# Two-step batches of VectorE's small work in a kernel's expert-row stage, with GpSimd's product ordered behind each batch

## The chip, the cores and the metric

The kernel runs on one core of one Trainium2 chip. The metric is the device time of one execution in microseconds (us); lower is better. The profile is one execution of its own, and its stretches are counted from the start of its span.

## The reference

The program is two transformer blocks, one after the other, on 256 tokens of width 2048, in 32-bit floats. The change lies in the feed-forward part of the first block, a mixture of 16,384 very small experts (`peer`). Each token has eight heads. A head has 128 scores for each of two key halves; it keeps the 16 best of each half, forms the 256 sums, and keeps the 16 best pairs. That gives 16 expert numbers and 16 gates (a softmax) for each of 256 tokens and eight heads. An expert is one row of 2048 numbers in `expert_down` and one in `expert_up`:

```python
expert_idx = jnp.take_along_axis(cand_i.reshape(T, H, K * K), best_pos, axis=-1)
gates = jax.nn.softmax(best_s, axis=-1).astype(x.dtype)
u = expert_down[ib]
act = jax.nn.gelu(jnp.einsum('td,thkd->thk', xb, u), approximate=False)
vv = expert_up[ib]
return jnp.einsum('thk,thkd->td', gb * act, vv)
```

So every token needs 128 rows of `expert_down`, a dot product of each with the token's own vector, a gelu, a multiplication by the gate (the result is called the coefficient here), and then a weighted sum of 128 rows of `expert_up`. The rest of the program (attention, retention, a second block with a grouped mixture of experts) is not touched.

## The kernel before, in words

128 tokens lie on the 128 partitions, so there are two token tiles (t = 0 and 1). The **down stage** is one Python loop of 128 steps `s`; a step is two of the sixteen experts of one head of one token tile, that is two down rows per token. The first 64 steps belong to tile 0, the other 64 to tile 1, eight steps to a head. Four streams of work meet in the loop.

- **Gathers** (`down_gather`, L628, on GpSimd's queue, POOL in the profile): two indirect DMAs per step, each bringing one row of 8 KB per token, 1 MB in all, into half of a buffer of the pool `big`. Step s issues the rows for three steps ahead (two after step 58). A gather waits until its buffer's last user is done.
- **Dot products** (`down_dots`): most rows go to VectorE (DVE), which multiplies a row by the token vector `hnp`, kept in PSUM, and sums it in one custom instruction (L669). In every second step (s even) the second row (numbers 1, 5, 9 and 13 of a head, `POOL_ROWS`) goes to GpSimd instead: it multiplies the row by the vector's copy `hn` in SBUF (L666), and ScalarE (ACT) sums the product later (`row_sum`, L642). Two steps, four rows, thus have one GpSimd product and three VectorE dots. Steps 0 to 7 and step 64 have no GpSimd product.
- **Routing** (`route`, L579 to L621): for each tile and head about 25 small VectorE instructions and one ScalarE exponential find the 16 experts. They are cut into eight pieces, 128 pieces for the 16 heads. `route_to(17 + int(ROUTE * s))` issues 1.41 pieces per step, so the last is issued near step 78.
- **Coefficient chunks** (`store_coefs`, 32 pieces from step 65 on): the coefficients of tile 0 are spread out to a table over experts. A piece takes four tokens: ScalarE builds one-hot rows (L694, L695), VectorE builds the coefficient side (`ab`, four instructions, L713), TensorE multiplies the two (L715), ScalarE copies the result (L716). Every eighth piece fills a chunk; three of the four are stored by a DMA that ScalarE issues (L767), and the chunk's buffer is one of those that rows use. `onehots_ahead` builds 28 more groups of one-hot rows on ScalarE from step 85 on. Per head ScalarE also takes the gelu (L646), and VectorE multiplies by the gates (L647).

In the program, step s calls gather, dots, then `settle` (work put off from the step before: the row sum, a head's coefficients), then its routing pieces and its piece of the tables. The text order is not the order on an engine: a scheduler fills each engine's queue by its own estimate of when an instruction can run. `tc.issue_after(x)` holds what follows back until instruction x has been issued in that order; it is no wait on the chip. Each engine then runs its own queue strictly in order, so an instruction that waits holds up all behind it. After the loop come the tables of tile 1 and the **up stage**, bound by TensorE.

Of the kernel before, what the change touches and what calls it, by code (L numbers as in the profile page):

```python
# [15 lines left out]
ALU = mybir.AluOpType  # L16
# [50 lines left out]
UA = 3  # L67
NC0 = 1
POOL_ROWS = (1, 5, 9, 13)
ROUTE = 1.41  # L70


def bc_rows(ap, n):
# [4 lines left out]
def build(ctx: ExitStack, tc: tile.TileContext, A, out, taps=None, stop=None):  # L78
    nc = tc.nc
    V, S, G, TE = nc.vector, nc.scalar, nc.gpsimd, nc.tensor  # L80
# [9 lines left out]
    env = {}  # L90
# [14 lines left out]
    def raw_tile(shape, name):  # L105
        p_ = env["raw"][env["ri"] % len(env["raw"])]
        env["ri"] += 1
        return p_.tile(shape, F32, tag="raw", name=name)
# [19 lines left out]
    def e8(shape, dt=F32, name="e8"):  # L128
        return env["wk"].tile(shape, dt, tag="e8", name=name, bufs=env["e8"])

    def bigt(shape, dt=F32, name="b"):
        return big.tile(shape, dt, tag="big", name=name)
# [175 lines left out]
    def pst(name="pst"):  # L308
        return pt.tile([P, 512], F32, tag="t", name=name)
# [171 lines left out]
    for b in range(4):  # L481
        ps = proj(5632 + b * 512)
        sg = w4([P, 2, 512], name="sg")
        for t in range(2):
            S.activation(sg[:, t, :], ps[:, t, :], AF.Silu, scale=r1[:, t:t + 1])
            V.tensor_tensor(out=ret[:, t, b * 512:(b + 1) * 512], in0=ret[:, t, b * 512:(b + 1) * 512],
                            in1=sg[:, t, :], op=ALU.mult)
# [62 lines left out]
    hn = bigt([P, 2, D], name="hn")  # L550
# [76 lines left out]
    def gather(dst, src, idx):  # L627
        G.indirect_dma_start(out=dst, out_offset=None, in_=src, in_offset=bass.IndirectOffsetOnAxis(ap=idx, axis=0))  # L628

    late = []  # L630

    def settle(n):

        while late and late[0][0] <= n:
            late.pop(0)[1]()

    def put_off(n, fn):
        late.append((n, fn))
        late.sort(key=lambda e: e[0])

    def row_sum(prod, dst):
        S.activation(prod, prod, AF.Copy, accum_out=dst)  # L642

    def peer_coefs(t, hd, dots):
        c_ = coef[:, t, hd * 16:(hd + 1) * 16]
        S.activation(c_, dots, AF.Gelu)  # L646
        V.tensor_tensor(out=c_, in0=c_, in1=gates[:, t, hd, :], op=ALU.mult)  # L647

    def down_gather(s):

        t, hd, k = s // 64, s // 8 % 8, s % 8 * 2
        row = bigt([P, 2, D], name="row")
        for i in range(2):
            gather(row[:, i, :], dn_d, eidx[:, t, hd, k + i:k + i + 1])
        rows[s] = row

    def down_dots(s, hnp):

        t, hd, k = s // 64, s // 8 % 8, s % 8 * 2
        if k == 0:  # L660
            rows["dots"] = sm.tile([P, 16], F32, tag="dots", name="dots")
        row, dots = rows.pop(s), rows["dots"]
        for i in range(2):
            r_, d_ = row[:, i, :], dots[:, k + i:k + i + 1]
            if hnp is not None and k + i in POOL_ROWS:
                G.tensor_tensor(out=r_, in0=r_, in1=hn[:, t, :], op=ALU.mult)  # L666
                put_off(s + 1, lambda r_=r_, d_=d_: row_sum(r_, d_))
            else:
                env["dot"] = V.tensor_tensor_reduce(out=r_, in0=r_, in1=hn[:, t, :] if hnp is None else hnp, scale=1.0,  # L669
                                                    scalar=0.0, op0=ALU.mult, op1=ALU.add, accum_out=d_)  # L670
        if k == 14:
            put_off(s + 1, lambda: peer_coefs(t, hd, dots))

    def key_rows(t):

        ps = pst("pky")
        for i in range(2):
            TE.transpose(ps[:, i * P:(i + 1) * P], ijf[:, t, i, :], ident)
        kT = env["wk"].tile([P, 2, P], F32, tag="brow", name="kT")
        V.tensor_copy(kT, ps[:, 0:2 * P].rearrange("p (a t) -> p a t", a=2))  # L680
        return kT
# [8 lines left out]
    def onehots(dst, kT, tk, n):  # L690


        for i in range(n):
            S.activation(dst[:, i, :], iota, AF.Square, scale=-1.0, bias=kT[:, 1, tk + i:tk + i + 1])  # L694
        S.activation(dst, dst, AF.Relu, scale=-1.0, bias=1.0)  # L695
# [46 lines left out]
    hnp = psum.enter_context(tc.tile_pool(name="hp", bufs=1, space=PSUM, reuse_waits="tile")).tile([P, D], F32, name="hnp")  # L742
    routed = [0]
# [9 lines left out]
    def route_to(n):  # L753

        while routed[0] < min(n, 128):
            next(route_pieces)
# [4 lines left out]
    def store_coefs():  # L761
        kT, cT = key_rows(0), coef_rows(0)
        for c in range(4):
            for cc_ in coef_chunk(kT, cT, c):
                yield
            if c < 4 - NC0:
                nc.scalar.dma_start(ct_d[c], cc_.rearrange("p i t -> p (i t)"))  # L767
            else:
                c0.append(cc_)

    def onehots_ahead(kT, oh1):

        for n, mk in ((16, lambda: raw_tile([P, 16, P], "oh1")), (16, lambda: raw_tile([P, 16, P], "oh1")),
                      (16, lambda: raw_tile([P, 16, P], "oh1")), (8, lambda: ws0.tile([P, 8, P], F32, tag="hi", name="oh1")),
                      (8, lambda: ws0.tile([P, 8, P], F32, tag="lo", name="oh1")),
                      (8, lambda: ws0.tile([P, 8, P], F32, tag="hi", name="oh1")),
                      (8, lambda: ws0.tile([P, 8, P], F32, tag="lo", name="oh1")),
                      (16, lambda: e8([P, 16, P], name="oh1")), (16, lambda: e8([P, 16, P], name="oh1"))):
            tk = 4 * len(oh1)
            o_ = mk()  # L780
            for q in range(0, n, 4):
                onehots(o_[:, q:q + 4], kT, tk + q, 4)
                oh1.append(o_[:, q:q + 4])
                yield

    kT1, oh1 = None, []
    stored = ahead = iter(())
    issued = 0
    route_to(16)
    for s in range(128):  # L790
        while issued < min(128, s + (4 if s < 58 else 3)):
            down_gather(issued)
            issued += 1
        if s in (6, 64):
            S.copy(hnp, hn[:, s // 64, :])
        down_dots(s, None if s < 8 or s == 64 else hnp)
        if s == 64:
            stored = store_coefs()
        settle(s)
        with tc.issue_after(env["dot"].ins):  # L800
            route_to(17 + int(ROUTE * s))
            if s > 64 and s % 3:
                next(stored, 1)
            if kT1 is None and routed[0] == 128:
                kT1 = key_rows(1)
                ahead = onehots_ahead(kT1, oh1)
            if s > 84 and s % 4:
                next(ahead, 1)
    settle(1000)
    for bg in (stored, ahead):  # L810
        for _ in bg:
# [454 lines left out]
    for pr in range(2):  # L1266
# [3 lines left out]
        for t in range(2):  # L1270
            for g in range(2 * pr, 2 * pr + 2):
# [5 lines left out]
                    in1=oh[:, :, :, None].to_broadcast([P, 2, 4, 8]), op=ALU.mult)  # L1277
# [261 lines left out]
```

## Time and profile before

| | us |
|---|---|
| median of 3 runs | 3273.74 |
| lowest and highest of them | 3271.95, 3275.97 |
| the profiled execution's own time | 3273.31 |
| its span | 3271.5 |
| VectorE busy | 2539.7 (78%) |
| GpSimd busy | 901.2 (28%) |
| ScalarE busy | 1659.8 (51%) |
| TensorE busy | 2553.7 (78%) |

The span in 40 slices of 82 us shows the down stage as the gap in TensorE's row: from about 900 to 1640 us TensorE is nearly idle, and GpSimd is busy nowhere else. Each digit is the busy share of a slice in tenths.

```
PE   9999999999800002222099999999999999999999
DVE  6665555455999999979788888888566699999984
ACT  5534444444422224673254444458444677777773
POOL 0000000000476775566776666640000000000000
DMA  7455555565898998899879999984654499999964
```

In such rows PE is TensorE, DVE VectorE, ACT ScalarE, POOL GpSimd; a row of the timeline gives start, duration, engine, line, operation and, in brackets, the engine's idle time just before and what ended it.

### The profile page before, as it was taken

To read this page: it belongs to the slowest core of one execution; us is meant where nothing else is said; L and a number is where in the kernel's file an instruction comes from. 1 tells how busy PE (TensorE), PEld (TensorE's weight loads), DVE (VectorE), ACT (ScalarE), POOL (GpSimd) and SP (SyncE) were. 2 spreads that over 40 slices of the span, in tenths; PEclk is the share of its full clock that TensorE was granted. 3 is DMA by queue.
4 is the path that set the end of the run, shared out by engine and by line. 5 is a ranking of instruction groups with operands and counts; after the bars stand their busy time and mean duration, and the time that the engine had idled before them with its cause. 6 is when DMAs were issued, how large, how long until landed. Compare 5 with 4: busy or idle time off the path is not lost. (4 is left out here: it accounts for less than half of the span.)

```text
span 3271.5 us, 35254 instructions
## 1 busy us (share of the span) xinstructions
PE 2553.7 (78%) x12368; PEld 2142.2 (65%) x12368; DVE 2539.7 (78%) x3564; ACT 1659.8 (51%) x2334; POOL 901.2 (28%) x634
## 2 busy tenths in 40 slices
PE   9999999999800002222099999999999999999999
PEld 7788888888800001111088888889987787878777
DVE  6665555455999999979788888888566699999984
ACT  5534444444422224673254444458444677777773
POOL 0000000000476775566776666640000000000000
PEclk9999999999955555555599999999999999999999
DMA  7455555565898998899879999984654499999964
GB/s 241 154 168 169 191 189 189 203 204 193 333 388 345 366 352 315 313 360 343 353 250 335 335 333 333 335 289 164 198 168 161 173 335 350 374 350 381 348 235 167
DMA packets 302521, 898.20 MB, mean 275 GB/s; under 512 B 20736, under 2 KB 42240, under 8 KB 268288
## 3 DMA queue, kind: packets, MB, share of 16 engines
q1 hardware_dynamic: 226560, 542.88, 47.2%
q0 software_dynamic: 57760, 335.65, 27.1%
q10 hardware_dynamic: 18016, 17.35, 1.6%
q8 instruction: 98, 1.61, 0.2%
q14 instruction: 87, 0.71, 0.1%
HBM read 887.42 MB, written 8.39 MB: 274 GB/s over the span
## 5 line engine op out<-in xcount | busy, mean ns | idle before, releaser
L262 DVE TENSOR_TENSOR wlo<-raw,whi 128x1024 fp32r<-128x1024 f32 (+1 forms) x538 | 647.9, 1207 | 448.3 <-ACT whi L261 441.7
L261 ACT CAST whi<-raw 128x1024 fp32r<-128x1024 f32 (+1 forms) x538 | 558.6, 1040 | 680.8 <-PE pj L292 255.9
L669 DVE CUSTOM_DVE_ANT_0 row<-row,hnp 128x2048 f32<-128x2048 f32 x179 | 403.8, 2278 | 38.2 <-DMA row<-in_peer_expert_down_dram,eidx 37.9
L207 POOL TENSOR_TENSOR r<-rstdv,mhalf 128x2 f32<-128x2 f32 x5 | 4.4, 889 | 1509.5 <-DVE rstdv L233 1509.5
L628 POOL DMA_INDIRECT urow<-in_peer_expert_up_dram,eidx x256 | 322.0, 1258 | 196.1 <-DVE h L838 139.7
L628 POOL DMA_INDIRECT row<-in_peer_expert_down_dram,eidx x256 | 264.2, 1032 | 307.0 <-DVE dots L669 85.0
L262 DVE TENSOR_TENSOR wlo<-rawg,whi 128x1024 fp32r<-128x1024 f32 x256 | 313.0, 1224 | 37.2 <-ACT whi L261 12.7
L261 ACT CAST whi<-rawg 128x1024 fp32r<-128x1024 f32 x256 | 269.8, 1055 | 99.1 <-PE pgu L1351 69.5
L290 PE MATMUL pj<-whi,xhi 128*128 128x512 f32 x736 | 289.4, 393 | 1.3 <-ACT whi L261 1.3
L291 PE MATMUL pj<-wlo,xhi 128*128 128x512 f32 x736 | 288.9, 393 | 0.0
L292 PE MATMUL pj<-whi,xlo 128*128 128x512 f32 x736 | 288.2, 392 | 0.0
L715 PE MATMUL pcc<-ab 128*128 128x128 f32 x288 | 76.0, 434 | 253.7 <-DVE ab L713 226.7
L666 POOL TENSOR_TENSOR row<-row,hn 128x2048 f32<-128x2048 f32 x59 | 266.6, 4519 | 4.6 <-DMA row<-in_peer_expert_down_dram,eidx 3.5
L715 PEld LDWEIGHTS pcc<-ab 128*128 128x128 f32 x288 | 63.2, 314 | 266.5 <-issue 166.6
L1350 PE MATMUL pgu<-wlo,xs 128*128 128x512 f32 x512 | 200.1, 391 | 3.1 <-DVE wlo L262 3.1
L1349 PE MATMUL pgu<-whi,xs 128*128 128x512 f32 x512 | 200.3, 391 | 0.0
L1351 PE MATMUL pgu<-whi,xs 128*128 128x512 f32 x512 | 199.4, 390 | 0.0
L838 DVE SCALAR_TENSOR_TENSOR h<-urow,pk,h 128x512 f32<-128x512 f32 x256 | 191.6, 748 | 4.4
L685 PE MATMUL pcf<-cc,pk 128*128 128x128 f32 x2 | 0.9, 474 | 248.0 <-DVE pk L647 248.0
L642 ACT ACTIVATE row<-row 128x2048 f32<-128x2048 f32 x59 | 112.2, 1903 | 143.4 <-POOL row L666 143.4
L262 DVE TENSOR_TENSOR wlo<-rawd,whi 128x1024 fp32r<-128x1024 f32 x128 | 154.0, 1223 | 12.2 <-ACT whi L261 1.1
L685 PEld LDWEIGHTS pcf<-cc,pk 128*128 128x128 f32 x2 | 0.4, 180 | 248.7 <-DVE pk L647 248.7
(552 smaller groups left out, 6842.4 us busy)
## 6 DMA issues: line engine op xcount, KB each, us to landing
raw<-in_w_in_dram SPq DMA_DIRECT2D x124, 1024.0 KB
raw<-in_peer_expert_up_dram SPq DMA_DIRECT2D x96, 1024.0 KB
rawg<-in_w_expert_gate_dram SPq DMA_DIRECT2D x128, 512.0 KB
rawg<-in_w_expert_up_dram SPq DMA_DIRECT2D x128, 512.0 KB
rawd<-in_w_expert_down_dram SPq DMA_DIRECT2D x64, 1024.0 KB
raw<-in_w_out_dram SPq DMA_DIRECT2D x32, 1024.0 KB
raw<-in_w_ret_branch_dram SPq DMA_DIRECT2D x16, 1024.0 KB
raw<-in_w_peer_query_dram SPq DMA_DIRECT2D x16, 1024.0 KB
```

What stands on the lines that cost most here:

```text
L261: S.copy(hi, raw)
L262: env["last"] = V.tensor_tensor(out=lo, in0=raw, in1=hi.bitcast(F32), op=ALU.subtract)
L290: TE.matmul(ps[:, t, :], h_, hi, start=st, stop=False)
L291: TE.matmul(ps[:, t, :], h_, lo, start=False, stop=False)
L292: env["mm"] = TE.matmul(ps[:, t, :], l_, hi, start=False, stop=en)
L628: G.indirect_dma_start(out=dst, out_offset=None, in_=src, in_offset=bass.IndirectOffsetOnAxis(ap=idx, axis=0))
L666: G.tensor_tensor(out=r_, in0=r_, in1=hn[:, t, :], op=ALU.mult)
L669: env["dot"] = V.tensor_tensor_reduce(out=r_, in0=r_, in1=hn[:, t, :] if hnp is None else hnp, scale=1.0, scalar=0.0, op0=ALU.mult, op1=AL ...
L838: V.scalar_tensor_tensor(out=h[:, t, 1536:2048], in0=row[:, k, :], scalar=coef[:, t, c0 + k:c0 + k + 1], in1=h[:, t, 1536:2048], op0=ALU.m ...
L1349: TE.matmul(o_, xh, hi[:, :, i, :], start=k == 0, stop=False)
L1350: TE.matmul(o_, xh, lo[:, :, i, :], start=False, stop=False)
L1351: TE.matmul(o_, xl, hi[:, :, i, :], start=False, stop=k == NK - 1)
```

## The change

Five things. In every even step but the first, the routing pieces of two steps are issued together (`ROUTE` is doubled and taken at s/2), with the table pieces of two steps behind them, and none in odd steps. This batch is held back until the last dot and the newest ScalarE instruction have been issued. The dots of a step are moved to the end of the step, behind the batch, and held back until the newest VectorE instruction has been issued. The second row of a step comes ahead of the first. And GpSimd's product gets a wait, on the chip, for the VectorE instruction that is newest where it is written.

```diff
-ROUTE = 1.41
+ROUTE = 2.82
...
-        for i in range(2):
+        for i in (1, 0):
             r_, d_ = row[:, i, :], dots[:, k + i:k + i + 1]
             if hnp is not None and k + i in POOL_ROWS:
-                G.tensor_tensor(out=r_, in0=r_, in1=hn[:, t, :], op=ALU.mult)
+                g_ = G.tensor_tensor(out=r_, in0=r_, in1=hn[:, t, :], op=ALU.mult)
+
+                tc.add_manual_dep(g_.ins, newest(V).name, mybir.DependencyInfo(
+                    mybir.DependencyClass.Sync, mybir.DependencyReason.DATA), reason="shared port")
                 put_off(s + 1, lambda r_=r_, d_=d_: row_sum(r_, d_))
...
-        down_dots(s, None if s < 8 or s == 64 else hnp)
         if s == 64:
             stored = store_coefs()
         settle(s)
-        with tc.issue_after(env["dot"].ins):
-            route_to(17 + int(ROUTE * s))
-            if s > 64 and s % 3:
-                next(stored, 1)
-            if kT1 is None and routed[0] == 128:
-                kT1 = key_rows(1)
-                ahead = onehots_ahead(kT1, oh1)
-            if s > 84 and s % 4:
-                next(ahead, 1)
+        if s and s % 2 == 0:
+            with tc.issue_after(env["dot"].ins), tc.issue_after(newest(S)):
+                route_to(18 + int(ROUTE * s / 2))
+                if kT1 is None and routed[0] == 128:
+                    kT1 = key_rows(1)
+                    ahead = onehots_ahead(kT1, oh1)
+                if s > 64:
+                    next(stored, 1)
+                    if s % 3 == 0:
+                        next(stored, 1)
+                if s > 84:
+                    next(ahead, 1)
+                    if s % 4 == 0:
+                        next(ahead, 1)
+        with tc.issue_after(newest(V)):
+            down_dots(s, None if s < 8 or s == 64 else hnp)
```

`newest(eng)` returns the last instruction written so far for that engine. By the new line numbers the VectorE dot is L676, GpSimd's product L670, the row sum L646, the gate product L651, `ab` L720.

On VectorE, in the first half of the loop (an `ISA` row with `row,dots` is a dot of 2048 elements, the `dots` row behind it reads its sum). Before, the small work of a head stands in every gap but the one inside a step of two VectorE dots:

```order
L587 CAST if_7131<-i_7108 128x32
L595 MAX bv<-rtmp 128x8
L596 MAX_INDEX bp<-bv,rtmp 128x8
L597 MATCH_REPLACE rtmp<-bv,rtmp 128x256
L669 ISA row,dots<-row,hnp 128x2048
L669 ISA dots 128x1
L599 MAX bv<-rtmp 128x8
L600 MAX_INDEX bp<-bv,rtmp 128x8
L602 TENSOR_SCALAR ab<-bp 128x16
L603 TENSOR_SCALAR ab<-bp 128x16
L605 CAST abf<-ab 128x32
L669 ISA row,dots<-row,hnp 128x2048
```

Now three dots stand in a row between two batches:

```order
L603 TENSOR_SCALAR ab<-bp 128x16
L605 CAST abf<-ab 128x32
L608 TENSOR_TENSOR rtmp<-abf,cc 128x512
L610 TENSOR_TENSOR rtmp<-rtmp,if_7134 128x512
L676 ISA row,dots<-row,hnp 128x2048
L676 ISA dots 128x1
L676 ISA row,dots<-row,hnp 128x2048
L676 ISA dots 128x1
L676 ISA row,dots<-row,hnp 128x2048
L676 ISA dots 128x1
L613 TENSOR_REDUCE pk<-rtmp 128x2x16
L617 TENSOR_SCALAR nm<-bv 128x1
```

The small instructions that stood between the first and the second dot have moved out; the same count of them now runs in one stretch ahead of the three dots.

On GpSimd, in the same part, with the waits (DMASW is a gather's landing). Before, the product waits for its row alone:

```order
L628 DMA row<-in_peer_expert_down_dram,eidx 128x2048 [waits DMASW3_49,DVE_49]
L628 DMA row<-in_peer_expert_down_dram,eidx 128x2048 [waits DMASW4_49]
L666 TENSOR_TENSOR row<-row,hn 128x2048 [waits DMASW6_49]
L628 DMA row<-in_peer_expert_down_dram,eidx 128x2048 [waits DMASW5_49,Activation_49]
L628 DMA row<-in_peer_expert_down_dram,eidx 128x2048
```

Now:

```order
L628 DMA row<-in_peer_expert_down_dram,eidx 128x2048 [waits DMASW3_49,DVE_49]
L628 DMA row<-in_peer_expert_down_dram,eidx 128x2048 [waits DMASW4_49]
L670 TENSOR_TENSOR row<-row,hn 128x2048 [waits DMASW6_49,DVE_49]
L628 DMA row<-in_peer_expert_down_dram,eidx 128x2048 [waits DMASW5_49,Activation_49]
L628 DMA row<-in_peer_expert_down_dram,eidx 128x2048
```

The places of product and gathers are the same; the product has one more wait, for VectorE, and the four gathers behind it stand behind that wait too.

## Rows read from the trace of the kernel before

**Rows 1.** Busy time by stretch: start:end, length, each engine's busy us, TensorE's clock, DMA share, GB/s.

```profile
904.00:1197.00 293.00, 0.66 (x2) 0.29 (x2) 289.02 (x453) 68.03 (x83) 209.74 (x124) 0.50 0.93 360
1197.00:1333.00 136.00, 21.70 (x73) 16.97 (x73) 133.75 (x258) 54.12 (x104) 80.44 (x50) 0.50 0.84 324
1333.00:1565.00 232.00, 49.24 (x186) 41.64 (x186) 192.26 (x209) 131.75 (x307) 151.57 (x91) 0.50 0.89 344
1585.00:1610.00 25.00, 0.00 (x0) 0.00 (x0) 17.05 (x16) 5.44 (x6) 21.34 (x12) 0.50 1.01 424
```

**Rows 2.** Timeline of GpSimd: the products of steps 8, 58, 78, 114 and 126.

```profile
904.06 4.53 POOL L666 TENSOR_TENSOR row<-row,hn 128x2048 f32<-128x2048 f32 x1
...
1197.04 4.53 POOL L666 TENSOR_TENSOR row<-row,hn 128x2048 f32<-128x2048 f32 x1
...
1333.79 4.50 POOL L666 TENSOR_TENSOR row<-row,hn 128x2048 f32<-128x2048 f32 x1
...
1565.22 4.53 POOL L666 TENSOR_TENSOR row<-row,hn 128x2048 f32<-128x2048 f32 x1
...
1623.86 4.51 POOL L666 TENSOR_TENSOR row<-row,hn 128x2048 f32<-128x2048 f32 x1 [2.92 <-DMA row<-in_peer_expert_down_dram,eidx]
```

**Rows 3.** Timeline of VectorE and GpSimd: a product beside small work, and a gather.

```profile
1010.40 4.64 DVE L587 CAST if<-i 128x32 f32<-128x32 uint32 x1
1010.48 4.51 POOL L666 TENSOR_TENSOR row<-row,hn 128x2048 f32<-128x2048 f32 x1
...
1022.67 1.46 POOL L628 DMA_INDIRECT row<-in_peer_expert_down_dram,eidx  x1 [0.30 <-issue]
```

**Rows 4.** Groups of VectorE, 904 to 1197 us: count | busy us, mean ns | idle before.

```profile
L621 DVE TENSOR_SCALAR pk<-pk,nm 128x16 f32<-128x16 f32 x8 | 15.8, 1972 | 0.1
L602 DVE TENSOR_SCALAR ab<-bp 128x16 uint32<-128x16 uint32 x9 | 14.1, 1570 | 0.3
L608 DVE TENSOR_TENSOR rtmp<-abf,cc 128x512 f32<-128x512 f32 x9 | 12.8, 1417 | 0.2
L587 DVE CAST if<-i 128x32 f32<-128x32 uint32 x9 | 11.2, 1245 | 0.0
L590 DVE TENSOR_TENSOR rtmp<-v 128x256 f32<-128x256 f32 x9 | 10.3, 1145 | 0.0
L614 DVE SCALAR_TENSOR_TENSOR eidx<-pk 128x16 int32<-128x16 f32 x8 | 8.7, 1082 | 0.0
L610 DVE TENSOR_TENSOR rtmp<-rtmp,if 128x512 f32<-128x512 f32 x9 | 6.2, 692 | 0.3
...
L597 DVE MATCH_REPLACE8 rtmp<-bv,rtmp 128x256 f32<-128x256 f32 x9 | 3.7, 409 | 0.0
L603 DVE TENSOR_SCALAR ab<-bp 128x16 uint32<-128x16 uint32 x9 | 1.7, 185 | 0.0
```

**Rows 5.** One line each, the dot and `ab`: ns min/median/max, first and last start.

```profile
L669 DVE CUSTOM_DVE_ANT_0 row<-row,hnp x179: 2262/2278/2289, 899.6 to 1628.7; 128x2048 f32<-128x2048 f32 x179
...
L713 DVE TENSOR_SCALAR ab<-cc,kT,cT x224: 322/340/5298, 1243.8 to 1664.5; 128x128 f32<-128x128 f32 x112
```

**Rows 6.** Groups of VectorE, 1197 to 1333 us.

```profile
L713 DVE TENSOR_SCALAR ab<-cc,kT,cT 128x128 f32<-128x128 f32 x37 | 24.0, 686 | 0.0
```

**Rows 7.** Groups of VectorE, 1333 to 1565 us.

```profile
L669 DVE CUSTOM_DVE_ANT_0 row<-row,hnp 128x2048 f32<-128x2048 f32 x53 | 119.3, 2278 | 18.0 <-DMA row<-in_peer_expert_down_dram,eidx 17.9
L713 DVE TENSOR_SCALAR ab<-cc,kT,cT 128x128 f32<-128x128 f32 x92 | 67.9, 800 | 0.0
...
L647 DVE TENSOR_TENSOR pk<-pk 128x16 f32<-128x16 f32 x5 | 4.7, 942 | 21.7 <-ACT pk L646 19.5 <-ACT row L642 2.2
```

**Rows 8.** Timeline of GpSimd: a gather behind a chunk's store, and the second gather of step 126.

```profile
1493.88 0.95 POOL L628 DMA_INDIRECT row<-in_peer_expert_down_dram,eidx  x1 [14.75 <-DMA ct_d<-cchunk]
...
1612.92 0.94 POOL L628 DMA_INDIRECT row<-in_peer_expert_down_dram,eidx  x1 [0.30 <-issue]
```

**Rows 9.** Timeline of GpSimd, ahead of the first product: a gather beside VectorE's weight splits.

```profile
869.43 2.94 POOL L628 DMA_INDIRECT row<-in_peer_expert_down_dram,eidx  x1 [7.06 <-DVE v L583]
```

More of the change, by code (lines that the diff above doesn't have):

```diff
@@ L628, in gather, with newest @@
         G.indirect_dma_start(out=dst, out_offset=None, in_=src, in_offset=bass.IndirectOffsetOnAxis(ap=idx, axis=0))
+    def newest(eng):
+        return next(i for i in reversed(nc.cur_bb.bb.instructions) if i.engine == eng.engine)
     late = []
```

## The prediction

> **What bounds the kernel now.** I read the stretches first. From 904 us (the first GpSimd product) VectorE is busy 289 of 293 us, then 133.75 of 136, while transfers run at 360 and 324 GB/s [rows 1]; late in the stage, where VectorE has little left, they run at 424 GB/s at a share of 1.01 [rows 1]. So until about step 78 VectorE sets the pace and the transfers have room. Second, the product starts, which are the stage's clock: one product per two steps, here called a round. Steps 8 to 58 are 25 rounds in 292.98 us, 11.72 each; steps 58 to 78 are 10 in 136.75, 13.68 each; steps 78 to 114 are 18 in 231.43, 12.86 each; steps 114 to 126 are 6 in 58.64, 9.77 each [rows 2]. The last figure is the best pace the stage shows. It is near what GpSimd alone needs: a product of 4.51 us and four gathers of 0.94 with 0.30 ahead of each, 9.47 [rows 2, 8].
>
> Third, what VectorE does in its busy time. A cast of 32 numbers begins at the end of a dot and takes 4.64 us; a product that began 0.08 us after it takes 4.51, and both end within 0.06 us [rows 3]. The same kind of work on 16 numbers takes 185 ns where it follows another of its kind [rows 4]. So VectorE is shown busy while it stands until GpSimd's product is over. The dots don't stand: 179 of them lie between 2262 and 2289 ns [rows 5], product or not. What stands can thus be counted, with the nearest undisturbed row as the true price: 185 ns for the small ones, 692 for 512 elements, 409 for 256 [rows 4]. L621 loses 15.8 - 8 x 0.185 = 14.3 us, L602 12.4, L608 6.6, L587 9.5, L590 6.6, L614 7.2: 56.6 us in steps 8 to 58, 2.26 a round. In steps 58 to 78 `ab` loses 24.0 - 37 x 0.340 = 11.4 us [rows 5, 6], in steps 78 to 114 67.9 - 92 x 0.340 = 36.6 us [rows 5, 7].
>
> **The change, part by part.** All is set against the profiled execution's 3273.31 us, which is 0.43 below the median of the runs.
>
> *The batch and the product's wait.* The product can now start only when a batch is over, and three dots follow the batch: 3 x 2.28 = 6.8 us of work that doesn't stand, over a product of 4.5 us [rows 2, 5]. The next batch meets the product only if it starts more than 2.3 us late. So nearly all of the 56.6, 11.4 and 36.6 us goes. What is late next differs by part.
>
> Steps 8 to 58: VectorE without its standing needs (292.98 - 56.6) / 25 = 9.46 us a round, GpSimd 9.47, the best pace shown is 9.77. Three cycles of nearly one length that wait for each other don't run at the longest one's pace, and batches are uneven (two or three pieces); I take 0.3 over it, 10.1. Gain 25 x (11.72 - 10.1) = 40 us. Bounds: 9.47 (56 us), and 11.0, one gather a round (1.24 us) pushed out of cover (18 us).
>
> Steps 58 to 78: VectorE carries routing and `ab`. It stays the bound at 13.68 - 1.14 = 12.5. Gain 11 us; bounds 0, if the batch waits for other engines instead, and 19, if routing's short instructions lose a third as much a round here as before (10 x 0.75) besides.
>
> Steps 78 to 114: VectorE needs (192.3 - 36.6) / 18 = 8.65 a round [rows 1], less than the pace of 9.77. So the full 36.6 can't be cashed by VectorE, but the round is now 12.86 for more reasons: VectorE also stood 21.7 us for ScalarE at L647 and 18.0 for rows [rows 7], and GpSimd's queue stood 14.75 us for a chunk's store [rows 8]. The one-hot work on ScalarE keeps its amount and is spread over more rounds; the wait for the store stays, since the gather that takes the chunk's buffer stands at the same kind of place. For three stores I leave about half of such a wait each, some 20 us or 1.1 a round: 10.9. Gain 18 x (12.86 - 10.9) = 35 us. Bounds: 9.77 (56 us) and 11.5 (24 us); the upper pace is worked out next.
>
> *What is queued behind the new wait.* Behind the product stand four gathers, and who waits for them is VectorE, one or two rounds later. With two rows ahead this closes a loop of four steps: product 4.5, the first gather's issue 1.24, landing of the second, two dots 4.6, a batch, the next product but one. The loaded landing can be read at the end of the stage: the second gather of step 126 is issued at 1612.92 and its product starts at 1623.86, 10.94 us [rows 2, 8]. With a batch of 8.65 - 6.8 = 1.8 us the loop takes 23.1 us for two rounds, 11.5 a round. That landing is mostly waiting behind other gathers, which shrinks when the pace drops, so I take it as the bound and not as the value. In steps 114 to 126 there is nearly no batch, but the product now waits for the dots before it: (23.1 - 1.8) / 2 = 10.6 against 9.77, at worst 5 us lost; I take 0.
>
> *The batch beside the gathers.* The small work no longer meets the product; it meets gathers. Within routing a gather beside VectorE's 512-element instructions took 1.46 us instead of 0.94 [rows 3, 8]. One such a round is 0.5 us on GpSimd, inside the 0.3 over pace and GpSimd's slack in steps 58 to 114; I add nothing.
>
> *The order pinned, row 1 ahead of row 0, steps 0 to 7.* The gather order stays 0 then 1, so in odd steps the first dot wants the row that lands last. Where rows are early this costs nothing; where they are late it is one transfer, 1 MB at 424 GB/s or 2.5 us per round, which the margin over 9.77 covers. Nothing for steps 0 to 7, where no product runs: 4 us either way.
>
> Sum: 40 + 11 + 35 = 86 us. 3273.3 - 86 = 3187 us.
>
> **The rivals.**
>
> *The transfers are the bound already.* VectorE would then wait for rows where it stood before. For it: a DMA share of 0.93 in steps 8 to 58 [rows 1]. Against: 424 GB/s in the last stretch, and VectorE busy in 289 of 293 us and 133.75 of 136 [rows 1], which leaves no room for waits on rows there. At today's 360 GB/s as a ceiling steps 8 to 58 gain nothing and the rest at most a few us: within 0.2%, 3270 us. [...]
>
> *The batch starves the gathers' issue; slower.* Ahead of the first product, where VectorE runs its 1024-element weight splits, a gather took 2.94 us [rows 9]. If a batch did that to gathers through a round, GpSimd would become the bound: over steps 8 to 126 the round is now (1623.86 - 904.06) / 59 = 12.20 us, and the change turns slower when the mean gather passes (12.20 - 4.51 - 1.20) / 4 = 1.62 us. At the middle of 0.94 and 2.94 a round is 4.51 + 4 x 2.24 = 13.5, 59 x 1.27 = 75 us more, 3348 us. Against: 1.46 was the most beside a 512-element instruction in the rows read, and a batch fills a third of a round (9.46 - 6.8 = 2.7 of some 10 us). [...]
>
> *Half the gain.* Batches end in waits of their own (the exponential behind L617, the gelu behind the dots), or the product starts so late that it still meets the next batch. For it: the 21.7 us that VectorE already stood at L647 [rows 7]; ScalarE's sums now wait behind a batch's one-hot rows. Then about half of each term, 20 + 5 + 16 = 41 us, 3232 us. Here too belongs that the change doesn't do what it says: the wait names the instruction newest in the program, and the scheduler may place others of the batch behind it, which then stand as before.
>
> *All of it.* The three lower bounds at once: 56 + 19 + 56 = 131 us, 3142 us.
>
> **How the numbers follow.** Forecast (3160 to 3215): 0.64. Half the gain (3215 to 3265): 0.16. All of it (below 3160): 0.09. Transfers bound: 0.05. Starved issue or another slower end: 0.06. A measurement of this kernel can tell about 0.2%, 6.5 us, from no change. So faster 0.88, same 0.05, slower 0.07. The range is 3145 to 3240 us: below, just short of the sum of the lower bounds, 3273 - 128; above, the upper ones with the tail's 5 us and the head's 4 against them, 18 + 0 + 24 - 9 = 33, 3273 - 33. It leaves out some 0.2.
>
> **What would show it.** L621, L602, L587 and `ab` at 0.2 to 0.4 us on average; rounds near 10 us up to step 58, and 11 after 78; VectorE with idle time ahead of dots, for rows, already before 1300 us; the product waiting for VectorE by a part of a us. Wrong would be: small instructions still at over 1 us (the wait doesn't hold), gathers of 1.5 us and more (starved issue), or the small instructions short and the rounds still near 11.7 (transfers).

## The result, and the profile after

The changed kernel takes 3190.57 us (median of 4 runs, 3189.34 to 3196.94) against 3273.62 for the kernel before: a ratio of 0.975, with a 95% interval of 0.9733 to 0.9767. The forecast was 3187 us, in a range of 3145 to 3240. The profiled execution took 3189.34 us, its span is 3187.6.

The product starts of the changed kernel, from GpSimd's timeline, are those of steps 8, 58, 78, 114 and 126 and answer to [rows 2]:

```profile
905.49 4.52 POOL L670 TENSOR_TENSOR row<-row,hn 128x2048 f32<-128x2048 f32 x1
...
1153.87 4.53 POOL L670 TENSOR_TENSOR row<-row,hn 128x2048 f32<-128x2048 f32 x1 [1.32 <-DVE rtmp L581]
...
1268.69 4.52 POOL L670 TENSOR_TENSOR row<-row,hn 128x2048 f32<-128x2048 f32 x1 [1.95 <-DVE ab L720]
...
1474.26 4.50 POOL L670 TENSOR_TENSOR row<-row,hn 128x2048 f32<-128x2048 f32 x1
...
1537.57 4.50 POOL L670 TENSOR_TENSOR row<-row,hn 128x2048 f32<-128x2048 f32 x1 [2.30 <-DMA row<-in_peer_expert_down_dram,eidx]
```

Taken apart as in the prediction, a round being two steps:

| steps | rounds | before, us a round | forecast | after | gain, forecast | gain, measured |
|---|---|---|---|---|---|---|
| up to 8 | | | | | 0 | -1.4 |
| 8 to 58 | 25 | 11.72 | 10.1 | 9.94 | 40 | 44.6 |
| 58 to 78 | 10 | 13.68 | 12.5 | 11.48 | 11 | 21.9 |
| 78 to 114 | 18 | 12.86 | 10.9 | 11.42 | 35 | 25.9 |
| 114 to 126 | 6 | 9.77 | 9.77 | 10.55 | 0 | -4.7 |

The sum of the measured gains is 86.3 us, at the product of step 126; the profiled executions differ by 84.0.

The stretches between these marks (busy us of TensorE, its weight loads, VectorE, ScalarE, GpSimd; clock, DMA share, GB/s) answer to [rows 1]:

```profile
905.00:1154.00 249.00, 0.66 (x2) 0.29 (x2) 235.62 (x471) 71.64 (x87) 208.38 (x125) 0.50 1.01 425
1154.00:1269.00 115.00, 21.19 (x78) 17.62 (x79) 113.48 (x234) 49.62 (x90) 82.39 (x50) 0.50 0.91 366
1269.00:1474.00 205.00, 45.12 (x183) 39.74 (x182) 156.70 (x209) 130.21 (x289) 149.62 (x90) 0.53 0.98 393
1474.00:1538.00 64.00, 0.00 (x0) 0.00 (x0) 39.12 (x36) 22.81 (x43) 48.69 (x30) 0.50 0.98 387
```

Up to step 58 the transfers went from 360 to 425 GB/s, a rate that [rows 1] showed only near the end of the stage; VectorE now has 13 us of slack there. From 58 to 78 it is VectorE that sets the pace, busy 113.5 of 115 us. The last two stretches are neither's: VectorE has 48 and 25 us of slack, and the transfers are below 425.

VectorE's groups between 905 and 1154 us (count, busy us, mean ns, idle before) answer to [rows 4]:

```profile
L608 DVE TENSOR_TENSOR rtmp<-abf,cc 128x512 f32<-128x512 f32 x9 | 6.2, 690 | 0.2
...
L590 DVE TENSOR_TENSOR rtmp<-v 128x256 f32<-128x256 f32 x8 | 3.3, 408 | 0.0
L621 DVE TENSOR_SCALAR pk<-pk,nm 128x16 f32<-128x16 f32 x9 | 2.2, 241 | 0.2
L602 DVE TENSOR_SCALAR ab<-bp 128x16 uint32<-128x16 uint32 x9 | 1.9, 214 | 0.3
L587 DVE CAST if<-i 128x32 f32<-128x32 uint32 x8 | 1.9, 239 | 0.0
...
L614 DVE SCALAR_TENSOR_TENSOR eidx<-pk 128x16 int32<-128x16 f32 x9 | 1.5, 167 | 0.2
```

The six groups that lost 56.6 us to GpSimd's product now take 17.0 us together, where they took 72.9. One round shows how, in the timeline of VectorE and then of GpSimd:

```profile
1005.01 0.16 DVE L614 SCALAR_TENSOR_TENSOR eidx<-pk 128x16 int32<-128x16 f32 x1
1005.10 2.28 DVE L676 CUSTOM_DVE_ANT_0 row<-row,hnp 128x2048 f32<-128x2048 f32 x1
...
1009.51 2.28 DVE L676 CUSTOM_DVE_ANT_0 row<-row,hnp 128x2048 f32<-128x2048 f32 x1
...
1005.40 4.54 POOL L670 TENSOR_TENSOR row<-row,hn 128x2048 f32<-128x2048 f32 x1
1010.10 0.98 POOL L628 DMA_INDIRECT row<-in_peer_expert_down_dram,eidx  x1 [0.16 <-issue]
```

The batch ends, the dots start, the product starts 0.3 us later and is over 1.8 us before the third dot is.

The waits of VectorE and GpSimd between 1269 and 1474 us (us in total, times, longest) show what holds steps 78 to 114:

```profile
DVE row L676 <- DMA row<-in_peer_expert_down_dram,eidx: 45.9, 15, 7.0
...
POOL row L628 <- DVE ab L720: 32.4, 16, 5.3
```

VectorE waits for rows while GpSimd's gathers wait for VectorE: each for the other, with transfers below their best rate, at 393 GB/s against 425. (These 16 gathers start about 0.3 us after the end of a dot; the trace names the instruction after it.)

### The profile page after: what moved, and what is told of

The parts are those of the page before. It is cut to its first block, busy times and chain, and to the rows that moved or that the text cites. A ratio compares the mean times of both kernels' runs of the same rounds, so it can differ in the third digit from the quotient of the medians.

```text
span 3187.6 us, 35309 instructions
## 1 busy us (share of the span) xinstructions
PE 2545.7 (80%) x12368; PEld 2136.7 (67%) x12368; DVE 2432.8 (76%) x3564; ACT 1667.5 (52%) x2336; POOL 899.2 (28%) x634
## 3 DMA queue, kind: packets, MB, share of 16 engines
q8 instruction: 99, 1.62, 0.2%
## 5 line engine op out<-in xcount | busy, mean ns | idle before, releaser
L676 DVE CUSTOM_DVE_ANT_0 row<-row,hnp 128x2048 f32<-128x2048 f32 x179 | 402.1, 2280 | 86.5 <-DMA row<-in_peer_expert_down_dram,eidx 84.1
L670 POOL TENSOR_TENSOR row<-row,hn 128x2048 f32<-128x2048 f32 x59 | 267.0, 4525 | 35.5 <-DVE ab L720 15.3
L646 ACT ACTIVATE row<-row 128x2048 f32<-128x2048 f32 x59 | 112.6, 1909 | 294.7 <-POOL row L670 294.7
```

Of the source, the lines that this page charges most:

```text
L670: g_ = G.tensor_tensor(out=r_, in0=r_, in1=hn[:, t, :], op=ALU.mult)
```

## The experiments

**The wait taken away.** All engines' orders stay as changed.

```diff
-                tc.add_manual_dep(g_.ins, newest(V).name, mybir.DependencyInfo(
-                    mybir.DependencyClass.Sync, mybir.DependencyReason.DATA), reason="shared port")
```

> The changed kernel without GpSimd's wait for the batch; the order on every engine stays the same. Theory (the gain comes from keeping VectorE's short instructions off GpSimd's product, and the wait does that): in the changed kernel GpSimd reaches the product at most 2 us before the batch ends, so without the wait the product starts beside the last short instructions and holds them for its 4.5 us; L621, L602, L587, L608 back at over 0.7 us on average, rounds of steps 8 to 58 at 11 us or more instead of 9.9, time above 3225 us. Rival (the order alone, three dots in a row, brings the gain): short instructions at 0.2 us but for a few, rounds within 0.3 of 9.9, time within 10 us of 3190.

Measured: 3255.71 us, ratio to before 0.9946 (0.993 to 0.9962). Rounds 11.49, 13.79, 11.82 and 10.49 us. VectorE's groups from 905 to 1191 us:

```profile
L614 DVE SCALAR_TENSOR_TENSOR eidx<-pk 128x16 int32<-128x16 f32 x9 | 32.0, 3558 | 0.2
L602 DVE TENSOR_SCALAR ab<-bp 128x16 uint32<-128x16 uint32 x9 | 20.6, 2284 | 0.3
L608 DVE TENSOR_TENSOR rtmp<-abf,cc 128x512 f32<-128x512 f32 x9 | 6.3, 696 | 0.2
```

The standing is back (L614 and L602 lose 49 us), in fewer groups than the expectation named: L608, L587 and L621 stay short. It is the instructions near the end of a batch that meet the product, since GpSimd comes to the product just then. Batching in this order is worth 17 us by itself; the wait is worth 65 on top.

**The wait alone, in the old order.**

```diff
-                G.tensor_tensor(out=r_, in0=r_, in1=hn[:, t, :], op=ALU.mult)
+                g_ = G.tensor_tensor(out=r_, in0=r_, in1=hn[:, t, :], op=ALU.mult)
+                tc.add_manual_dep(g_.ins, newest(V).name, mybir.DependencyInfo(
+                    mybir.DependencyClass.Sync, mybir.DependencyReason.DATA), reason="shared port")
```

> The kernel before with the product's wait for the newest VectorE instruction alone, its order untouched. Theory: in the old order half of a round's short work stands behind the product's first dot, 2.2 us after the product's start, so it still meets the product; stands of 1.5 to 2.5 us each instead of up to 4.6, rounds of steps 8 to 58 at 11 to 12 us, time 3240 to 3290 us. Rival (the wait alone brings the gain): rounds near 10, time below 3215 us.

(`newest` is defined as in the change.) Measured: 3282.89 us, ratio 1.0031 (1.0021 to 1.0042), 0.3% slower than before; rounds 11.86, 14.41, 12.79 and 9.73. L602 stands at 1784 ns on average, L614 at 1426, L590 at 1311. So neither half brings the gain: the wait sets when the product starts, and only the three dots behind it make the next 4.5 us a time in which hardly anything can stand. 17 us and -10 us apart, 83 together.

**Rows in the order of their landing in odd steps.**

```diff
-        for i in (1, 0):
+        for i in ((0, 1) if s % 2 else (1, 0)):
```

> The changed kernel with row 0 ahead of row 1 again in odd steps, as the gathers land; even steps as changed. Theory (after step 58, with two rows ahead, the rounds of 11.4 and 10.6 us are a loop: gather, landing, dots, batch, product, gather; the dot that wants the row landing last lengthens it): the first odd dot starts up to 2.4 us earlier, VectorE's waits for rows after step 78 (46 + 25 us) shrink by a third or more, rounds 0.5 to 1.2 us shorter after step 78, time 3165 to 3182 us. Rival (VectorE needs both rows before it goes on, so the loop closes over the later of the two either way): the dots end when the last row has landed plus one dot instead of two, at most; if GpSimd's issue sets the pace, no change within 5 us.

Measured: 3165.20 us, ratio to before 0.9668 (0.9654 to 0.9682), 25 us below the change. The product starts of steps 78, 114 and 126:

```profile
1268.10 4.53 POOL L670 TENSOR_TENSOR row<-row,hn 128x2048 f32<-128x2048 f32 x1 [1.95 <-DVE ab L720]
...
1458.82 4.52 POOL L670 TENSOR_TENSOR row<-row,hn 128x2048 f32<-128x2048 f32 x1
...
1516.94 4.51 POOL L670 TENSOR_TENSOR row<-row,hn 128x2048 f32<-128x2048 f32 x1 [2.98 <-DVE dots L676]
```

Rounds of 10.60 and 9.69 us instead of 11.42 and 10.55, and 9.93 and 11.37 before them, as with the change. The transfers of steps 78 to 114:

```profile
1268.00:1459.00 191.00, 45.85 (x185) 40.23 (x184) 156.79 (x210) 130.23 (x289) 150.46 (x91) 0.52 1.01 424
```

424 GB/s where the change has 393, and VectorE's waits for rows after step 78 fall from 70.5 to 45.3 us. So the reversed order in the 64 odd steps costs 25 us, nearly all of it where rows are issued only two steps ahead.

**No wait from step 114 on.**

```diff
-                tc.add_manual_dep(g_.ins, newest(V).name, mybir.DependencyInfo(
-                    mybir.DependencyClass.Sync, mybir.DependencyReason.DATA), reason="shared port")
+                if s < 114:
+                    tc.add_manual_dep(g_.ins, newest(V).name, mybir.DependencyInfo(
+                        mybir.DependencyClass.Sync, mybir.DependencyReason.DATA), reason="shared port")
```

> The changed kernel with the product's wait only up to step 112; from step 114 on, where no short work is left, the product waits for its row alone as before the change. Theory (there the wait is for the dots of the step before and closes the loop): rounds of steps 114 to 126 go back from 10.6 to 9.8 us, 5 us less, time 3184 to 3188 us. Rival (the order of the rows or the spread one-hot work makes the end slower): rounds stay at 10.5, no change.

Measured: 3193.73 us, ratio 0.9758 (0.9744 to 0.9771); rounds of steps 114 to 126 at 10.55, as with the change. The theory's mechanism for the end falls: the product's wait for the dots of the step before costs nothing there. With the row order mended the same rounds take 9.69, so it is the order that costs.

**VectorE's dots from SBUF.** The dot reads the token vector from `hn`, as GpSimd does, and not from `hnp` in PSUM.

```diff
-                env["dot"] = V.tensor_tensor_reduce(out=r_, in0=r_, in1=hn[:, t, :] if hnp is None else hnp, scale=1.0,
+                env["dot"] = V.tensor_tensor_reduce(out=r_, in0=r_, in1=hn[:, t, :], scale=1.0,
```

> The changed kernel with VectorE's dots reading the token vector from SBUF (hn) instead of PSUM (hnp); the results are the same. Theory (what stands beside GpSimd's product is an instruction of VectorE that takes part of SBUF's way that GpSimd uses; the dot goes free only because one of its two inputs lies in PSUM): dots now collide, either a dot lasts up to 6.8 us or the product does; mean of dot or product up by more than 1 us, rounds of steps 8 to 58 at 12 us or more, time above 3300 us. Rival (only short instructions stand, for a reason of their own, such as their start): dots stay at 2.28 and products at 4.5 us, time within 15 us of 3190.

Measured: 3368.53 us, ratio 1.029 (1.0273 to 1.0308). In the timeline, GpSimd and VectorE:

```profile
1000.39 2.46 POOL L628 DMA_INDIRECT row<-in_peer_expert_down_dram,eidx  x1 [0.30 <-issue]
...
1001.97 2.28 DVE L676 CUSTOM_DVE_ANT_0 row<-row,hn 128x2048 f32<-128x2048 f32 x1
1002.86 5.75 POOL L670 TENSOR_TENSOR row<-row,hn 128x2048 f32<-128x2048 f32 x1
...
1005.35 5.40 DVE L676 CUSTOM_DVE_ANT_0 row<-row,hn 128x2048 f32<-128x2048 f32 x1
```

Now the product stands for the dot that began before it, the next dot stands for the product, and gathers stand too: between 905 and 1150 us a gather takes 1.82 us on average, where the changed kernel's take 0.96, and a product 5.14. With the same instruction and tile, and nearly the same order, the place of one operand decides: the changed kernel's dots that read the vector from PSUM take 2.26 to 2.29 us, product or not, and the dots here up to 7.24. What the two engines share there is not shown.

**Rows issued two steps ahead in the first half too.** The gathers of steps 0 to 57 come two steps ahead instead of three.

```diff
-        while issued < min(128, s + (4 if s < 58 else 3)):
+        while issued < min(128, s + 3):
```

> The changed kernel with the gathers of steps 0 to 57 issued two steps ahead instead of three, as after step 58. Theory (the 11.4 and 10.6 us rounds after step 78 are a loop over gather, landing and dots that has one row less of slack): steps 8 to 58 become as slow, 10.5 to 11.5 us a round instead of 9.9, 15 to 40 us more in all, with VectorE's waits for rows there rising from 9 us to 30 or more. Rival (the slow rounds after 78 come from the tables: ScalarE's one-hot rows and the chunk stores): steps 8 to 58 stay within 0.3 us of 9.9.

Measured: 3221.26 us, ratio 0.9839 (0.9818 to 0.9861). Steps 8 to 58 take 11.25 us a round, the rest is as with the change (11.72, 11.43, 10.63). VectorE waits 23 us for rows there instead of 9, fewer than expected; between 905 and 1154 us the product also waits 41 us for its batch, where the changed kernel's waits 13. So rounds of 11.2 us come about without tables or stores, as soon as rows in this order are issued only two steps ahead. How much of the 1.3 us is due to the row order there is not shown, since no run has the mended order two steps ahead in this part.

**No one-hot rows ahead.** The four lines that build tile 1's one-hot rows in the loop are left out, so all 28 groups are built behind it.

> The changed kernel with no one-hot rows of tile 1 built inside the loop; they are all built behind it, so the whole gets longer by up to 61 us. What counts is steps 78 to 114. Theory (loop of gathers): rounds stay at 11.0 to 11.5 us. Rival (ScalarE's one-hot work delays TensorE, that the next `ab`, that the batch and the product): rounds fall to 10.5 us or less.

Measured: one time, 3206.02 us. Steps 78 to 114 take 12.15 us a round, more than with the change, which neither theory had. The scheduler had filled ScalarE's queue in another order: two rounds took 18.1 and 17.8 us, with VectorE standing 10.9 us for a gelu and a gather 8.51 us for a chunk's store; the other sixteen average 11.4. That speaks against ScalarE's one-hot work as the limit, but the run changed more than one thing and settles it only together with the two runs on the order and the lead of the rows above.

**No product at all, in the kernel before.**

```diff
-POOL_ROWS = (1, 5, 9, 13)
+POOL_ROWS = ()
```

> The kernel before with no product on GpSimd at all: VectorE takes all four dots of a round. Theory (the product alone makes the short instructions stand): L621, L602, L587, L614 and `ab` at 0.16 to 0.35 us on average; rounds of steps 8 to 58 at 4 x 2.2 + 2.7 = 11.5 us against 11.72 now, so that the stage is hardly slower without GpSimd's help: time 3255 to 3290 us. Rival (they stand for the gathers' issue as well): averages stay above 0.5 us and the time rises above 3300 us.

Measured: 3220.68 us, ratio 0.984 (0.9824 to 0.9857). VectorE's groups, 905 to 1197 us, and the one line of `ab` (ns min/median/max):

```profile
L621 DVE TENSOR_SCALAR pk<-pk,nm 128x16 f32<-128x16 f32 x9 | 2.1, 229 | 0.2
L602 DVE TENSOR_SCALAR ab<-bp 128x16 uint32<-128x16 uint32 x9 | 1.9, 215 | 0.2
...
L713 DVE TENSOR_SCALAR ab<-cc,kT,cT x224: 327/342/550, 1242.0 to 1613.0; 128x128 f32<-128x128 f32 x112
```

The averages are as the theory had them, and the time is 34 us below its lower end. GpSimd's help cost the kernel before 53 us. It took 59 of the 256 rows, 135 us of VectorE's work at 2.28 us each, and none of that was saved, as the stretch from 860 us to the start of the last dot shows, in the kernel before and in this run:

```profile
860.00:1629.00 769.00, 104.06 (x525) 90.23 (x523) 701.34 (x1032) 284.48 (x531) 519.37 (x307) 0.53 0.90 351
...
860.00:1577.00 717.00, 102.99 (x525) 90.03 (x523) 700.91 (x1150) 174.66 (x416) 245.44 (x248) 0.53 0.95 376
```

VectorE is busy 701 us either way: what the help took off it came back, in the main as standing. The 53 us are its idle time, 68 us with the help and 16 without. The changed kernel takes 30 us less than this run, but whether the help pays in the changed order is not shown: that order was not run without the product.

**Tables later, on top of the mended row order.**

```diff
-        while issued < min(128, s + (4 if s < 58 else 3)):
+        while issued < min(128, s + (4 if s < 72 else 3)):
...
-                if s > 64:
+                if s > 78:
                     next(stored, 1)
```

> The changed kernel with rows 0, 1 in odd steps, the coefficient tables of tile 0 begun at step 80 instead of 66, and the third row ahead kept to step 71 instead of 57. Theory (with the row order mended, steps 8 to 58 and 114 to 126 run at the transfers' pace of 9.7 to 9.9 us a round, and only steps 58 to 78 are still VectorE's, at 11.4, because routing and tables fall together there): steps 58 to 78 fall to 10.0 to 10.5 us a round (10 us less), steps 78 to 126 stay within 0.4 us a round of 10.6 and 9.7, time 3150 to 3162 us. Rival (steps 58 to 78 are bound by the shorter look-ahead or by the vector copy at step 64): less than 4 us gained, or the tables end late and the stage's end is later.

Measured: 3160.24 us, ratio 0.9657 (0.9644 to 0.967). Steps 58 to 78 fall to 10.11 us a round, 12.6 us less than with the row order alone; steps 78 to 126 give 5.5 us of it back (10.68 and 10.35). Two things were changed here, the start of the tables and the lead of the rows up to step 71, and which of them gave the gain is not shown. The interval overlaps that of the row order alone, so 5 us between the two are not settled; both beat the change.

**Row 1's gather first in even steps**, on the mended row order.

```diff
-        for i in range(2):
+        for i in ((0, 1) if s % 2 else (1, 0)):
             gather(row[:, i, :], dn_d, eidx[:, t, hd, k + i:k + i + 1])
```

> The changed kernel with rows 0, 1 in odd steps, and in even steps the gather of row 1, GpSimd's, issued ahead of row 0's. Theory (the loop after step 78 closes over whichever row is late): the product, which waits for rows 8.5 us in all with the order 0, 1, would wait less, but VectorE's first dot of the even step gets its row 2.4 us later, and VectorE already waits 54 us for rows: no gain, 0 to 10 us slower than 3165. Rival (the product's start sets the loop): rounds of steps 78 to 114 below 10.4 us, time below 3160 us.

Measured: 3164.91 us, ratio 0.9674 (0.9661 to 0.9687); rounds 9.99, 11.39, 10.56 and 9.37. No difference that can be told from the row order alone. After step 78 the product no longer waits for its row, 8.5 us in all with the row order alone, and the time stays. In even steps VectorE and GpSimd take one row each, and it does not matter here which is issued first (3164.91 us against 3165.20).

## Why the prediction was right, and where its steps were off

*What bounds the kernel* was read rightly. VectorE's short instructions stood until GpSimd's product was over; three runs show it from three sides. Without the wait the standing comes back at the end of each batch (L614 at 3558 ns on average), without the product it is gone (L621 at 229, L602 at 215), and with the dot's second operand in SBUF the dots stand as well (up to 7.24 us).

*Steps 8 to 58* (10.1 us a round, bound by three cycles of nearly one length): 9.94, at 425 GB/s. The allowance of 0.3 over the best pace came out at 0.17.

*Steps 58 to 78* (gain 11 us): 21.9. The mechanism was right, VectorE is the bound, and `ab` fell from 24.0 to 12.6 us, by the 11.4 us counted. Of the rest a good part lies in the marks. VectorE's groups between 1197 and 1333 us before, and between 1154 and 1269 us after:

```profile
L669 DVE CUSTOM_DVE_ANT_0 row<-row,hnp 128x2048 f32<-128x2048 f32 x34 | 76.5, 2276 | 0.0
...
L676 DVE CUSTOM_DVE_ANT_0 row<-row,hnp 128x2048 f32<-128x2048 f32 x30 | 67.5, 2278 | 1.0 <-DMA row<-in_peer_expert_down_dram,eidx 0.8
L720 DVE TENSOR_SCALAR ab<-cc,kT,cT 128x128 f32<-128x128 f32 x40 | 12.6, 344 | 0.0
```

In the kernel before, the gathers ahead of step 78's product waited for a chunk's store, which the prediction had left out of this part; GpSimd's timeline:

```profile
1331.10 0.94 POOL L628 DMA_INDIRECT row<-in_peer_expert_down_dram,eidx  x1 [13.19 <-DMA ct_d<-cchunk]
```

That wait is not among the changed kernel's. VectorE went on meanwhile, so between the same two products it ran 9 us more of dots than it does now, work that belongs to the steps beside this part. By this estimate some 13 of the 21.9 us were gained here. What the store's wait itself cost is not shown by a run.

*Steps 78 to 114* (10.9): 11.42, gain 25.9 instead of 35. Two errors meet here. The 1.1 us a round left for the chunk stores was not needed: none of the changed kernel's gathers waits for a store between 1269 and 1474 us. And the loop over gather, landing, dots and batch, worked out at 11.5 us a round and set aside as a bound, was the value. The prediction's reason for setting it aside, that the landing gets shorter when the pace drops, did not save it.

*Steps 114 to 126* (9.77, at worst 10.6): 10.55, nearly the bound again. Here the prediction had named the wrong part of the change, the product's wait for the dots before it; with that wait taken away nothing changes.

*The step that failed* is the one on the pinned order: row 1 ahead of row 0 in odd steps was to cost "nothing", since the margin over 9.77 would cover a row landing 2.5 us later. There was no margin. With rows issued two steps ahead, a gather waits for a buffer, the buffer for the dots of its last row, and these dots for the row that lands last; VectorE then has both dots still to do. In the order of landing it does one of them while the other row comes in, and a round is 0.8 to 0.9 us shorter: 14.9 us in steps 78 to 114 and 5.2 in the last six rounds, of 21.3 by which the two profiled executions differ (25 by the medians). Up to step 58, where rows are issued three steps ahead, the order costs nothing (9.93 against 9.94). The prediction's own loop, 23.1 us for two rounds, becomes 10.4 us a round with one dot less, by estimate; 10.60 was measured.

So it was partly luck that the sum came out (86.3 against 86 us at step 126, the whole within 4 us): 14 us more gain before step 78 than forecast, and 14 less after it, cancel. Some of both is only the late mark at step 78; the loss by the row order is real.

*The rivals.* Transfers as the bound: not at 360 GB/s, which rose to 425 and stayed there over 249 us. Starved issue: the changed kernel's gathers take 0.96 us on average between 905 and 1154 us, below 1.62. The starved gather exists, though, beside dots with both operands in SBUF: 1.82 us on average, in the one run that is clearly slower than before. This is also what [rows 9] shows. The prediction put that gather of 2.94 us down to VectorE's weight splits; but from 869.28 to 871.55 us VectorE runs a dot that reads `hn` in SBUF, as all dots of steps 0 to 7 do, and the gather ends 0.82 us after it:

```profile
869.28 2.27 DVE L669 CUSTOM_DVE_ANT_0 row<-row,hn 128x2048 f32<-128x2048 f32 x1
```

So the rival's price was taken from an instruction that a batch doesn't contain. Half the gain: the instructions that the scheduler leaves behind the product are there, but few. L621 behind a dot stood 2.4 us in three rounds of steps 58 to 78, and L651 3.9 us in two rounds of steps 78 to 114.

```profile
L621 DVE TENSOR_SCALAR pk<-pk,nm 128x16 f32<-128x16 f32 x3 | 7.2, 2405 | 0.1
```

All of it, 3142 us: no run came there; with the row order mended and the tables later it is 3160.

## What to carry to other kernels

When a short VectorE instruction shows a mean far above its minimum, look at what GpSimd runs at its start and end; if they end together, as L602's 5.14 us and the product's 4.51 did within 0.04 us of each other in the run without the wait, the price is standing as it was here, and either give GpSimd's work a stretch in which VectorE runs only instructions whose times don't change beside it (here the dots from PSUM, 2.26 to 2.29 us), or ask by a run without it whether the help pays at all. An order and a wait may each bring little alone, so try them together before dropping either. Use rows in the order in which they land, above all where few are in flight: a bound worked out for a loop of waits deserves belief where few rows are in flight (here 11.5 us a round worked out, 11.42 measured, with rows issued two steps ahead).

## What the runs showed of the hardware that had not been expected

An instruction that stands can have begun before the product: in the kernel before, between 904 and 1197 us, 14 instructions of VectorE other than dots took over 0.9 us and ended within 0.05 us of a product's end, and 3 of them began ahead of that product, by 0.08 to 0.55 us. The cast of [rows 3] started 0.08 us ahead of it, and in the run without the wait L602 started 0.59 us ahead and still ended with it, at 1013.0. GpSimd's timeline there shows why:

```profile
1007.51 0.95 POOL L628 DMA_INDIRECT row<-in_peer_expert_down_dram,eidx  x1 [0.30 <-issue]
1008.48 4.51 POOL L670 TENSOR_TENSOR row<-row,hn 128x2048 f32<-128x2048 f32 x1
```

and VectorE's:

```profile
1007.89 5.14 DVE L602 TENSOR_SCALAR ab<-bp 128x16 uint32<-128x16 uint32 x1
```

It began within a gather's issue, which ends at 1008.46; the product followed 0.02 us later and VectorE did not get in between. That a gather alone can hold a short instruction is shown by the run without the product. There L602 began 0.63 us into a gather of 0.94, took 0.30 us and ended with it:

```profile
1016.75 0.94 POOL L628 DMA_INDIRECT row<-in_peer_expert_down_dram,eidx  x1 [3.86 <-DVE dots L669]
...
1017.38 0.30 DVE L602 TENSOR_SCALAR ab<-bp 128x16 uint32<-128x16 uint32 x1
```

At 1051.92, 0.17 us into a gather, it took 0.17 us. So not every instruction that begins within a gather is held, and what decides is open, since the one above was held though it began 0.38 us into its gather. That gather and product hold VectorE in one and the same way is inferred from these times and not shown by a run of its own.
